# mLSTM values of two heads projected with tokens on partitions, the doubling operand of the delta-rule solve placed behind the low parts of the weights, longer pauses in the mixers

## Chip, cores and metric

One core of one Trainium2 chip runs the whole kernel. The metric is device time in microseconds (us) of one execution; the median of several runs is compared. TensorE (PE) does matmuls and transposes, VectorE (DVE), ScalarE (ACT) and GpSimd (POOL) do the element work, SyncE (SP) issues the DMAs.

## What is computed

One decoder layer on 1024 tokens of width 1024, all in float32: RMSNorm, one combined input projection, three causal token mixers in parallel (gated DeltaNet with 4 heads, mLSTM with 4 heads, native sparse attention with 8 heads), their output projections, merge gates, an output projection, a SwiGLU feed-forward part and a gated per-layer embedding. The part that the change touches most, the mLSTM of a head (cut):

```
qk = einsum('nbhid,nbhjd->nbhij', qc, kc)          # chunks of 64 tokens
Sm = exp(D_ - mt[..., None]) * qk_                 # decays and gates
num = si[..., None] * (q_ @ Cb) + Sm @ v_          # values v enter here
den = si * (q_ . nb) + sum(Sm, -1)
h  = num / max(|den|, exp(-mt))[..., None]
Cb = sc * Cb + wk^T @ v_                           # and here: state matrix
...
h = rms_f32(h, norm_w) * sigmoid(o_pre)
```

and of the gated DeltaNet the triangular solve `T = (I + X)^-1` with `u = T @ (v*beta)`, `w = T @ (k*beta*exp(g))`, the scan over chunks, and `rms_f32(o, norm_w) * silu(z)`.

## The kernel before

**Products.** A float32 product is made of three matmuls in a rounded float32 format: with each operand split into a high part and the rest (low part), high by high, high by low, low by high. The activations are split once per stage. The weights are streamed in blocks of four tiles of 128x512 (`run_blocks`, L404): SP fetches `wraw` two blocks ahead, ACT copies it to the high part `whi` (L434), POOL subtracts to get the low part `wlo` (L436), with five buffers for each. While block i is multiplied, the parts of block i+1 are made.

**Two forms of a block.** `chan_block` (L484) keeps a 128x128 piece of weights as the stationary operand and streams 512 tokens: the result has channels on partitions. A block is 2 column tiles x 2 halves of the tokens x 8 steps of the depth x 3 = 96 matmuls of 512 columns. `tok_block` keeps 128 tokens as the stationary operand and streams 256 columns of weights: the result has tokens on partitions, 8 token tiles x 8 x 3 = 192 matmuls of 256 columns. Both write to the two PSUM banks called `mm`, in turn, and an eviction empties a bank after each 24 matmuls.

**Mixers woven in.** Between two steps of a block (`advance`), generators of the mixers are moved on: `scans()` (`gdn_scan` of the four heads) and `side()` (the gates, `gdn_solve` of four heads, `mls_side` of four heads, with tables of the attention after the second). Each `yield` is such a place. `pause(us)` lets a generator sit out so much of woven time, in which the projections go on (a step counts 1.4 us). `behind()` ties a group of PE instructions behind the last matmul of the block so far. A scheduler then puts the instructions in order, so that the order on an engine is not simply that of the code.

**Stages of the profiled execution** (us): set-up to 60; DeltaNet heads' projections, with solves and scans beside them, to some 450; mLSTM heads to some 740; projections for the attention to 890; attention to 1290; branch and output projections to 1500; feed-forward and embedding to the end.

**What the change's steps touch.**
- `gates` side: `m_crow` (L749) is a running maximum on DVE; PE transposes it (`mtr2`; the trace writes `mtr`).
- `gdn_solve`: after the substitution on DVE, blocks of 16x16 go through DRAM (`xds`, L964, and back to `zd`, L967), and POOL spreads one of them into `gV` (L974), DVE the other into `gW`; then come the doubling steps on PE (`levq`, `levv`, `levw`).
- `gdn_scan`, its end: the sums of squares give `rsqrt` (a chain of tiny DVE operations on 128x8, L298 to L302), two DVE multiplications on `vtok` (L1078), a pause, two groups of four PE transposes (`gytr`), and DVE multiplies by the gate (L1085).
- `mls_blocks` (L1093): two channel blocks a head, (q, k) and (v, o), evicted by ACT (L1104, L1106).
- `mls_side` (L1113): row broadcasts `mrb` on PE from diagonals `mrb_d` that POOL makes (L813); `mE` is made by DVE (L1125), POOL (L1126) and ACT (exp, L1127), and multiplied on DVE (L1136) by `mqk` from PE; `mktr` are transposes of k, from which DVE makes `mwk` (L1141). The values come with channels on partitions, so PE transposes them in two groups of four (`mvtr`, L1147) and ACT copies the results to `mva` (L1149), which has a 129th column of ones. Then eight chunks of `mops` and `mups` (matmuls of 129 columns), the norm, a pause, and transposes `mytr`.

Of the kernel before, what the change touches and what calls it, by code (L numbers as in the profile page):

```python
# [11 lines left out]
F32 = mybir.dt.float32  # L12
F32R = mybir.dt.float32r
I32 = mybir.dt.int32
AF = mybir.ActivationFunctionType
# [121 lines left out]
def _blocks(w_in, w_branch, w_out, w_ffn_in, w_ffn_out, w_ple_gate, w_ple_proj):  # L137
    out = []

    def cols(w, *cs):  # L140
        out.append(np.concatenate([_rows(w[:, c:c + n]) for c, n in cs], 2).reshape(P, -1))
# [15 lines left out]
    for h in range(4):  # L157
        c = 2056 + 128 * h
        cols(w_in, (c, 128), (512 + c, 128))
        cols(w_in, (1024 + c, 128), (1536 + c, 128))  # L160
# [61 lines left out]
def bc(ap, shape):  # L222
    return ap.to_broadcast(list(shape))
# [8 lines left out]
class Trunk:  # L232
# [170 lines left out]
    def run_blocks(self, blocks, rate, both=0, first=None, fetch=None):  # L403
# [21 lines left out]
        def halve(i):  # L425
            if i < n:
                parts = self.raw.pop(i)
                if len(blocks[i]) > 2:
                    parts = blocks[i][2](parts)
                self.wsplit[i] = []  # L430
                for t in parts:
                    hi = self.wpool.tile([P, 512], F32R, tag="whi", name="whi", bufs=W_BUFS[1])
                    lo = self.wpool.tile([P, 512], F32R, tag="wlo", name="wlo", bufs=W_BUFS[1])
                    nc.scalar.activation(hi, t, AF.Copy)  # L434
                    eng = nc.vector if len(blocks[i]) == 2 and len(self.wsplit[i]) % 2 < both else nc.gpsimd
                    eng.tensor_tensor(lo, t, hi.bitcast(F32), OP.subtract)  # L436
                    self.wsplit[i].append((hi, lo))
# [235 lines left out]
    def gates_side(self):  # L673
# [76 lines left out]
        yield from self.pause(2.0)  # L750
# [113 lines left out]
    def gdn_solve(self, h):  # L864
# [107 lines left out]
        V, W = r3(self.b2("gV")), r3(self.b2("gW"))  # L972
        for eng, M, w in ((nc.gpsimd, V, 0), (nc.vector, W, 1)):
            eng.tensor_tensor(M.rearrange("p t (d i) -> p t d i", d=4), bc(d3(1 + w).unsqueeze(2), [P, NT, 4, 16]),  # L974
                              bc(self.blk4.unsqueeze(1).unsqueeze(3), [P, NT, 4, 16]), OP.mult)
        yield from self.pause(24.0)
# [50 lines left out]
    def gdn_scan(self, h):  # L1027
# [51 lines left out]
        yield from self.pause(8.0)  # L1079
# [13 lines left out]
    def mls_blocks(self, h):  # L1093
        nc = self.nc
        st = self.ml[h] = {}

        def evac(which):
            def f(ct, hf, ps):
                n = which[ct]
                sl = slice(hf * 512, hf * 512 + 512)  # L1100
                if hf == 0:
                    st[n] = self.a4("m" + n, tag="x")
                if n == "o":
                    nc.scalar.activation(st[n][:, sl], ps, AF.Tanh, scale=0.5)  # L1104
                else:
                    nc.scalar.activation(st[n][:, sl], ps, AF.Copy, scale=128 ** -0.5 if n == "k" else 1.0)  # L1106
                if hf == 1:
                    self.flags.add(("m", h, n))
            return f

        return [(self.chan_block(self.u, evac("qk")), None), (self.chan_block(self.u, evac("vo")), None)]

    def mls_side(self, h):  # L1113
        nc = self.nc
        st = self.ml[h]
# [13 lines left out]
        yield  # L1129
# [14 lines left out]
        va = self.a4("mva")[:, :].rearrange("p (t c) -> p t c", c=129)  # L1144
        nc.gpsimd.memset(va[:, :, 128:129], 1.0)
        for hf in H:
            with self.behind():  # L1147
                ps = self.four_tr(st["v"][:, hf * 512:hf * 512 + 512], "mvtr")
            nc.scalar.activation(va[:, 4 * hf:4 * hf + 4, 0:128], t4(ps[:, :]), AF.Copy)  # L1149
            yield  # L1150
# [38 lines left out]
        yield from self.pause(6.0)  # L1189
# [864 lines left out]
    def build(self, stages="ABCNRF"):  # L2054
# [23 lines left out]
        with tc.tile_pool(name="small", bufs=1) as self.spool, tc.tile_pool(name="mix", bufs=1) as self.apool, \  # L2078
                tc.tile_pool(name="halves", bufs=1) as self.bpool, tc.tile_pool(name="stage", bufs=2) as self.stage:
            self.setup()  # L2080
            with tc.tile_pool(name="ps1", bufs=1, space=MS) as self.psum:
# [5 lines left out]
                for h in range(4):  # L2087
                    blocks += self.mls_blocks(h)
# [52 lines left out]
```

## Time and profile before

| | |
|---|---|
| median of 3 runs | 2320.23 us (2319.97 to 2320.33) |
| the profiled execution, its own time | 2323.84 us |
| span of its trace | 2322.1 us |
| mean granted TensorE clock | 0.993 |
| PE busy | 2260.9 us, 97% of the span |
| DVE, ACT, POOL busy | 1325.0 (57%), 851.4 (37%), 732.2 (32%) |
| chain that ended last | PE 83%, DVE 11%, issue 3%, ACT 2%, others about 1% |

How to read it: the busy shares say which engine has the least room. The chain that ended last is followed back from the last instruction, at each step to what released it; its share of an engine is time that the end hangs on. The granted clock is the share of full speed that TensorE was given in a stretch; it has two levels, 1.2 and 2.4 GHz. A timeline row has the start, the length and the operation of a run of equal instructions; in brackets stands how long the engine sat idle before it and what released it. Starts of PE rows are exact to the hundredth shown; the ends are modelled and overlap the next row, so a rate on PE is read from start to start.

### The profile page before, as it was taken

What the parts mean: (1) busy time and instruction counts of PE and PEld (TensorE: products, weight loads), DVE (VectorE), ACT (ScalarE), POOL (GpSimd) and SP (SyncE); (2) the same over time, 40 slices, a digit from 0 to 9 for tenths busy, and PEclk for the clock granted to TensorE, in tenths of its full rate; (3) what the DMA queues carried; (4) which work ended last, traced back from release to release, by engine and by line L of the source; (5) the groups of instructions that cost most, each with busy time, mean ns of one, the idle gap of its engine ahead of it and who ended that gap; (6) DMA issues with size and microseconds to landing.
All of it is one profiled execution on the core that took longest, in us unless ns stands there. A gap on an engine that the chain in (4) does not pass through costs nothing.

```text
span 2322.1 us, 32707 instructions
## 1 busy us (share of the span) xinstructions
PE 2260.9 (97%) x12032; PEld 1796.5 (77%) x12032; DVE 1325.0 (57%) x3050; ACT 851.4 (37%) x1817; POOL 732.2 (32%) x616
## 2 busy tenths in 40 slices
PE   8999999999999999999999999999999999999999
PEld 6777778788778996667667777777888888888877
DVE  5445554644223446888883456587555555555584
ACT  6423232423322335555553323453222222222362
POOL 2343434332222123221222151214334444344412
PEclk9999999999999999999999999999999999999999
DMA  6130312121222132111103653311111111111134
GB/s 229 51 107 28 107 38 89 46 62 37 82 70 82 46 109 96 51 60 37 37 33 106 221 185 128 123 55 47 54 50 51 53 52 50 50 51 55 55 124 144
DMA packets 115111, 182.93 MB, mean 79 GB/s; under 512 B 24523, under 2 KB 34420, under 8 KB 114952
## 3 DMA queue, kind: packets, MB, share of 16 engines
q1 hardware_dynamic: 114664, 180.71, 22.9%
q8 instruction: 95, 1.56, 0.3%
q14 instruction: 64, 0.52, 0.1%
q10 hardware_dynamic: 288, 0.14, 0.0%
HBM read 149.04 MB, written 31.76 MB: 78 GB/s over the span
## 4 chain that ended last, share of the span: by engine, by line
PE 83%; DVE 11%; issue 3%; ACT 2%; DMA 1%; POOL 1%; SPq 0%; ACTq 0%; DVEq 0%; POOLq 0%
PE mm L247 67%; PE nso L247 3%; PE ptr L255 2%; PE S L247 2%; DVE P L1553 1%; PE mops L247 1%; PE gks L247 1%; PE gram L247 1%; PE gpu L247 1%; DVE P L1542 1%; POOL wlo L436 0%; DVE wlo L436 0%; DVE xn L1803 0%; DVE kT L852 0%; PE levv L247 0%
## 5 line engine op out<-in xcount | busy, mean ns | idle before, releaser
L436 POOL TENSOR_TENSOR wlo<-wraw,whi 128x512 fp32r<-128x512 f32 x334 | 446.8, 1344 | 1016.3 <-ACT whi L434 786.1
L247 PE MATMUL mm<-u,whi 128*128 128x512 f32 x1888 | 629.7, 408 | 3.9 <-ACT mg L1682 2.1
L434 ACT ACTIVATE whi<-wraw 128x512 fp32r<-128x512 f32 x408 | 255.9, 630 | 430.0 <-PE mm L247 339.5
L247 PEld LDWEIGHTS mm<-u,whi 128*128 128x128 f32 x1888 | 346.6, 191 | 77.4 <-issue 5.2
L247 PE MATMUL mm<-u,wlo 128*128 128x512 f32 x928 | 374.8, 404 | 3.6 <-POOL wlo L436 3.6
L247 PEld LDWEIGHTS mm<-u,wlo 128*128 128x128 f32 x928 | 176.0, 190 | 41.5 <-POOL wlo L436 4.1
L1921 DVE TENSOR_TENSOR fc<-fc,mm 128x512 f32<-128x512 f32 x140 | 95.2, 686 | 156.2 <-PE mm L247 156.2
L1962 DVE TENSOR_TENSOR xt<-xt,mm 128x512 f32<-128x512 f32 x176 | 118.2, 684 | 55.9 <-PE mm L247 54.6
L247 PE MATMUL mm<-whi,alo 128*128 128x512 f32 x352 | 140.7, 400 | 0.0
L247 PE MATMUL mm<-whi,ahi 128*128 128x512 f32 x352 | 139.8, 397 | 0.6 <-DVE xt L1962 0.5
L247 PE MATMUL mm<-wlo,ahi 128*128 128x512 f32 x352 | 139.5, 396 | 0.0
L436 POOL TENSOR_TENSOR wlo<-ws,whi 128x512 fp32r<-128x512 f32 x60 | 85.1, 1418 | 150.4 <-ACT whi L434 150.4
L247 PE MATMUL mm<-u2lo,whi 128*128 128x512 f32 x304 | 120.6, 397 | 0.0
L247 PE MATMUL mm<-u2hi,whi 128*128 128x512 f32 x304 | 120.3, 396 | 0.0
L247 PE MATMUL mm<-u2hi,wlo 128*128 128x512 f32 x304 | 119.7, 394 | 0.0
L436 DVE TENSOR_TENSOR wlo<-wraw,whi 128x512 fp32r<-128x512 f32 x74 | 68.7, 928 | 77.4 <-ACT whi L434 77.2
L1548 ACT ACTIVATE P<-P,n_ng 128x640 f32<-128x640 f32 (+7 forms) x128 | 92.8, 727 | 54.0 <-DVE n_ng L1546 53.5
L434 ACT ACTIVATE whi<-ws 128x512 fp32r<-128x512 f32 x60 | 37.8, 630 | 167.2 <-DVE xt L1962 114.7
L255 PE MATMUL ptr<-ident,P 128*128 128x128 f32 x528 | 88.2, 280 | 8.2 <-DVE P L1553 7.5
L247 PE MATMUL mm<-whi,u 128*128 128x256 f32 x512 | 94.3, 283 | 0.0
L255 PEld LDWEIGHTS ptr<-ident,P 128*128 128x128 f32 x528 | 60.6, 140 | 40.1 <-DVE P L1553 13.0
L247 PEld LDWEIGHTS mm<-whi,alo 128*128 128x128 f32 x352 | 66.3, 188 | 18.7 <-DVE alo L1878 3.1
(506 smaller groups left out, 4711.4 us busy)
## 6 DMA issues: line engine op xcount, KB each, us to landing
wraw<-in_w_dram SPq DMA_DIRECT2D x408, 256.0 KB, 2.5
mgs<-mg SPq DMA_DIRECT2D x48, 256.0 KB, 2.2
mgld<-mgs SPq DMA_DIRECT2D x48, 256.0 KB, 5.4
xt<-in_x_dram SPq DMA_DIRECT2D x8, 512.0 KB, 5.8
xt<-in_x_dram SPq DMA_DIRECT2D x16, 256.0 KB, 6.1
pg<-pps SPq DMA_DIRECT2D x16, 256.0 KB, 3.8
out_dram<-sg SPq DMA_DIRECT2D x15, 256.0 KB, 2.5
pps<-ppst SPq DMA_DIRECT2D x8, 256.0 KB, 2.0
```

The source lines that it names most:

```text
L247: return self.nc.tensor.matmul(out, lhsT, rhs, start=start, stop=stop).ins
L255: self.nc.tensor.transpose(out, in_, self.ident[:n, :n])
L434: nc.scalar.activation(hi, t, AF.Copy)
L436: eng.tensor_tensor(lo, t, hi.bitcast(F32), OP.subtract)
L1542: nc.vector.tensor_tensor_reduce(pt[:, farw:nk], sp2[:, farw - cut:nk - cut], near[g][:, n % 2], 1.0, -3e38, OP.add, OP.max, mx[:, n, 1:2])
L1548: nc.scalar.activation(pts[i][:, :nk], pts[i][:, :nk], AF.Exp, bias=ng[:, i:i + 1], accum_out=sm[:, g, i % 2:i % 2 + 1])
L1553: nc.vector.tensor_scalar(pts[i][:, :nk], pts[i][:, :nk], sm[:, g, i % 2:i % 2 + 1], gate[:, g, i % 2:i % 2 + 1], OP.mult, OP.mult)
L1921: nc.vector.tensor_tensor(t, x, ps, OP.add)
L1962: nc.vector.tensor_tensor(self.h[tt][s], self.h[tt][s], ps, OP.add)
```

## The change

- `mls_blocks` takes a pair of heads. Its blocks are (q, k of the first), (values of both), (o of both), (q, k of the second) in place of (q, k), (v, o), (q, k), (v, o). The values' block is a `tok_block`: tokens on partitions, 256 columns for two heads. Its results are copied by ACT straight into `mva` of either head, 128x128 each, two for a token tile. The transposes `mvtr` and the copies behind them are gone. The host's packing of the weights follows the same order.
- `run_blocks` remembers the last low part that POOL was given (`last_lo`), and `gdn_solve` issues `gV` behind it; its pause of 24 is split into 10 before `gV` and `gW`, and 14 after.
- Pauses: before the transposes of `m_crow` 2 to 5, before `gytr` 8 to 12, before `mqk` one step to 6, before `mytr` 6 to 11.

```diff
@@ -1,5 +1,5 @@
 import math
-from contextlib import ExitStack, contextmanager
+from contextlib import ExitStack, contextmanager, nullcontext
 
 import numpy as np
 
@@ -154,10 +154,12 @@
         cols(w_in, (1024 + c, 128), (1536 + c, 128))
         for b in _MG[h]:
             gates(b)
-    for h in range(4):
+    for h in (0, 2):
         c = 2056 + 128 * h
         cols(w_in, (c, 128), (512 + c, 128))
-        cols(w_in, (1024 + c, 128), (1536 + c, 128))
+        cols(w_in, (1024 + c, 256))
+        cols(w_in, (1536 + c, 256))
+        cols(w_in, (128 + c, 128), (640 + c, 128))
     for c in (4624, 4880, 5136, 4112, 4368):
         cols(w_in, (c, 256))
     for b in _MG[4]:
@@ -433,7 +435,9 @@
                     lo = self.wpool.tile([P, 512], F32R, tag="wlo", name="wlo", bufs=W_BUFS[1])
                     nc.scalar.activation(hi, t, AF.Copy)
                     eng = nc.vector if len(blocks[i]) == 2 and len(self.wsplit[i]) % 2 < both else nc.gpsimd
-                    eng.tensor_tensor(lo, t, hi.bitcast(F32), OP.subtract)
+                    low = eng.tensor_tensor(lo, t, hi.bitcast(F32), OP.subtract)
+                    if eng is nc.gpsimd:
+                        self.last_lo = low.ins
                     self.wsplit[i].append((hi, lo))
 
         self.raw, self.wsplit = {}, {}
@@ -747,7 +751,7 @@
         nc.vector.tensor_copy(srow, ps[:32, :P])
         crow = self.b2("m_crow")[:32, :P]
         nc.vector.tensor_tensor_scan(crow, srow, srow, -3e38, OP.max, OP.max)
-        yield from self.pause(2.0)
+        yield from self.pause(5.0)
         ps = self.ps("mtr2")
         with self.behind():
             self.tr(ps[:, :32], crow)
@@ -970,10 +974,14 @@
         ch = lambda m, c: m[64 * (c % 2):64 * (c % 2) + 64, c // 2]
         r3 = lambda t: t[:, :].rearrange("p (t c) -> p t c", c=64)
         V, W = r3(self.b2("gV")), r3(self.b2("gW"))
+        yield from self.pause(10.0)
         for eng, M, w in ((nc.gpsimd, V, 0), (nc.vector, W, 1)):
-            eng.tensor_tensor(M.rearrange("p t (d i) -> p t d i", d=4), bc(d3(1 + w).unsqueeze(2), [P, NT, 4, 16]),
-                              bc(self.blk4.unsqueeze(1).unsqueeze(3), [P, NT, 4, 16]), OP.mult)
-        yield from self.pause(24.0)
+
+            with self.tc.issue_after(self.last_lo) if w == 0 else nullcontext():
+                eng.tensor_tensor(M.rearrange("p t (d i) -> p t d i", d=4),
+                                  bc(d3(1 + w).unsqueeze(2), [P, NT, 4, 16]),
+                                  bc(self.blk4.unsqueeze(1).unsqueeze(3), [P, NT, 4, 16]), OP.mult)
+        yield from self.pause(14.0)
 
         VV = t4(self.a4("gVV")[:, :S])
         nc.gpsimd.memset(VV[64:128, :, 0:64], 0.0)
@@ -1076,7 +1084,7 @@
         for hf in H:
             sl = slice(hf * 512, hf * 512 + 512)
             nc.vector.tensor_tensor(t4(o[:, sl]), t4(o[:, sl]), hd(f, hf), OP.mult)
-        yield from self.pause(8.0)
+        yield from self.pause(12.0)
         yT = self.a4("gyT")
         for hf in H:
             sl = slice(hf * 512, hf * 512 + 512)
@@ -1091,28 +1099,41 @@
 
 
     def mls_blocks(self, h):
-        nc = self.nc
-        st = self.ml[h] = {}
-
-        def evac(which):
+
+
+        nc = self.nc
+        st = [self.ml.setdefault(h + i, {}) for i in range(2)]
+
+        def evac(names):
             def f(ct, hf, ps):
-                n = which[ct]
+                n, i = names[ct]
                 sl = slice(hf * 512, hf * 512 + 512)
                 if hf == 0:
-                    st[n] = self.a4("m" + n, tag="x")
+                    st[i][n] = self.a4("m" + n, tag="x")
                 if n == "o":
-                    nc.scalar.activation(st[n][:, sl], ps, AF.Tanh, scale=0.5)
+                    nc.scalar.activation(st[i][n][:, sl], ps, AF.Tanh, scale=0.5)
                 else:
-                    nc.scalar.activation(st[n][:, sl], ps, AF.Copy, scale=128 ** -0.5 if n == "k" else 1.0)
+                    nc.scalar.activation(st[i][n][:, sl], ps, AF.Copy, scale=128 ** -0.5 if n == "k" else 1.0)
                 if hf == 1:
-                    self.flags.add(("m", h, n))
+                    self.flags.add(("m", h + i, n))
             return f
 
-        return [(self.chan_block(self.u, evac("qk")), None), (self.chan_block(self.u, evac("vo")), None)]
+        def values(tt, _, ps):
+            for i in range(2):
+                if tt == 0:
+                    va = st[i]["v"] = self.a4("mva")[:, :].rearrange("p (t c) -> p t c", c=129)
+                    nc.gpsimd.memset(va[:, :, 128:129], 1.0)
+                nc.scalar.activation(st[i]["v"][:, tt, 0:128], ps[:, i * P:i * P + P], AF.Copy)
+                if tt == NT - 1:
+                    self.flags.add(("m", h + i, "v"))
+
+        chan = lambda *names: (self.chan_block(self.u, evac(names)), None)
+        return [chan(("q", 0), ("k", 0)), (self.tok_block(self.utok, values), None), chan(("o", 0), ("o", 1)),
+                chan(("q", 1), ("k", 1))]
 
     def mls_side(self, h):
         nc = self.nc
-        st = self.ml[h]
+        st = self.ml.setdefault(h, {})
         H = range(2)
         t4 = lambda ap: ap.rearrange("p (t c) -> p t c", c=P)
         hd = lambda ap, hf: bc(ap[:, 4 * hf:4 * hf + 4].unsqueeze(2), [P, 4, P])
@@ -1126,7 +1147,7 @@
             nc.gpsimd.tensor_tensor(t4(E), t4(E), bc(self.cmask.unsqueeze(1), [P, 4, P]), OP.add)
             nc.scalar.activation(E, E, AF.Exp)
             sms.append(E)
-        yield
+        yield from self.pause(6.0)
         for hf in H:
             ps = self.ps("mqk")
             with self.behind():
@@ -1141,13 +1162,7 @@
             nc.vector.tensor_tensor(t4(wk[:, hf * 512:hf * 512 + 512]), t4(ps[:, :]), hd(self.mwks[:, :, h], hf), OP.mult)
             yield
         yield from self.need(("m", h, "v"))
-        va = self.a4("mva")[:, :].rearrange("p (t c) -> p t c", c=129)
-        nc.gpsimd.memset(va[:, :, 128:129], 1.0)
-        for hf in H:
-            with self.behind():
-                ps = self.four_tr(st["v"][:, hf * 512:hf * 512 + 512], "mvtr")
-            nc.scalar.activation(va[:, 4 * hf:4 * hf + 4, 0:128], t4(ps[:, :]), AF.Copy)
-            yield
+        va = st["v"]
         C = self.small("mC", [P, 129], bufs=2)
         nc.gpsimd.memset(C, 0.0)
         num = self.a4("mnum")[:, :].rearrange("p (t c) -> p t c", c=129)
@@ -1186,7 +1201,7 @@
         for hf in H:
             sl = slice(hf * 512, hf * 512 + 512)
             nc.vector.tensor_tensor(t4(y[:, sl]), num[:, 4 * hf:4 * hf + 4, 0:128], hd(f, hf), OP.mult)
-        yield from self.pause(6.0)
+        yield from self.pause(11.0)
         yT = self.a4("myT")
         for hf in H:
             sl = slice(hf * 512, hf * 512 + 512)
@@ -2084,7 +2099,7 @@
                 for h in range(4):
                     blocks += self.gdn_blocks(h)
                     blocks += [self.mg_block(b, 0) for b in _MG[h]]
-                for h in range(4):
+                for h in (0, 2):
                     blocks += self.mls_blocks(h)
                 blocks += self.nsa_blocks()
                 blocks += [self.mg_block(b, 0) for b in _MG[4]]
```

In the changed file the same lines stand 2 to 15 lines lower. How it moves instructions is shown at three places.

POOL, at the first solve's `gV`, before. The four tiles `wlo_1444` to `wlo_1456` are the low parts of one block of weights, `wlo_1524` the first of the next:

```order
L436 TENSOR_TENSOR wlo_1444<-wraw_1316,whi_1443 128x512 [waits DMAHW0_49,PE_49,Activation_49]
L436 TENSOR_TENSOR wlo_1448<-wraw_1318,whi_1447 128x512 [waits DMAHW4_49,PE_49,Activation_49]
L436 TENSOR_TENSOR wlo_1452<-wraw_1320,whi_1451 128x512 [waits DMAHW5_49,PE_49,Activation_49]
L974 TENSOR_TENSOR gV_1424<-zd_1366,c128_135 128x512 [waits DMAHW3_49]
L436 TENSOR_TENSOR wlo_1456<-wraw_1322,whi_1455 128x512 [waits DMAHW6_49,PE_49,Activation_49]
L436 TENSOR_TENSOR wlo_1524<-wraw_1459,whi_1523 128x512 [waits DMAHW0_49,PE_49,Activation_49]
L813 TENSOR_TENSOR gcb_d_1780<-ident_87,cumhi_785 128x512 [waits DVE_49,PE_49]
```

and with the change (there the four are `wlo_1442` to `wlo_1454`):

```order
L438 TENSOR_TENSOR wlo_1442<-wraw_1316,whi_1441 128x512 [waits DMAHW0_49,PE_49,Activation_49]
L438 TENSOR_TENSOR wlo_1446<-wraw_1318,whi_1445 128x512 [waits DMAHW4_49,PE_49,Activation_49]
L438 TENSOR_TENSOR wlo_1450<-wraw_1320,whi_1449 128x512 [waits DMAHW5_49,PE_49,Activation_49]
L438 TENSOR_TENSOR wlo_1454<-wraw_1322,whi_1453 128x512 [waits DMAHW6_49,PE_49,Activation_49]
L981 TENSOR_TENSOR gV_1424<-zd_1366,c128_135 128x512 [waits DMAHW3_49]
L438 TENSOR_TENSOR wlo_1524<-wraw_1457,whi_1523 128x512 [waits DMAHW0_49,PE_49,Activation_49]
L817 TENSOR_TENSOR gcb_d_1780<-ident_87,cumhi_785 128x512 [waits DVE_49,PE_49]
```

The fourth low part now goes ahead of `gV`, which waits for a DMA in both orders.

PE, at the end of the first head's scan, before. `mm_2157` and `mm_2234` are projection banks, `ktr` transposes of the next head:

```order
L247 MATMUL mm_2157<-u_600,whi_1535 128x512 x2
L247 MATMUL mm_2157<-u_600,wlo_1536 128x512
L247 MATMUL mm_2157<-u_618,whi_1535 128x512 x2
L247 MATMUL mm_2157<-u_618,wlo_1536 128x512
L255 MATMUL gytr_2198<-ident_87,vtok_1757 128x128 [waits DVE_49,Activation_49]
L255 MATMUL gytr_2198<-ident_87,vtok_1757 128x128 x3
L255 MATMUL gytr_2204<-ident_87,vtok_1757 128x128 [waits DVE_49]
L255 MATMUL gytr_2204<-ident_87,vtok_1757 128x128 x3
L247 MATMUL mm_2234<-u_301,whi_1874 128x512 x2
```

with the change (the end of what now goes ahead of `gytr`; `mm_2221` is the bank after `mm_2157`, and three of its triples of matmuls and the first matmul of a fourth stand before this piece):

```order
L257 MATMUL ktr_2176<-ident_87,gq_1912 128x128 [waits Activation_49]
L257 MATMUL ktr_2176<-ident_87,gq_1912 128x128 x3
L249 MATMUL mm_2221<-u_334,whi_1878 128x512
L249 MATMUL mm_2221<-u_334,wlo_1879 128x512
L249 MATMUL mm_2221<-u_382,whi_1882 128x512 x2
L249 MATMUL mm_2221<-u_382,wlo_1883 128x512 [waits Pool_49]
L249 MATMUL mm_2221<-u_390,whi_1882 128x512 x2
L249 MATMUL mm_2221<-u_390,wlo_1883 128x512
L257 MATMUL gytr_2262<-ident_87,vtok_1757 128x128 [waits DVE_49]
L257 MATMUL gytr_2262<-ident_87,vtok_1757 128x128 x3
L257 MATMUL gytr_2268<-ident_87,vtok_1757 128x128 [waits DVE_49]
L257 MATMUL gytr_2268<-ident_87,vtok_1757 128x128 x3
```

Between the last matmul of `mm_2157` and the first `gytr` there was nothing, and now there are 18 matmuls of the next bank and the four `ktr` transposes. At the second head 21 matmuls and four transposes are moved ahead in the same way.

PE, at the running maximum in the gates' side, before:

```order
L255 MATMUL mtr_804<-ident_87,m_s_802 32x128 [waits DVE_49,Activation_49]
L247 MATMUL mm_848<-u_468,wlo_639 128x512
L247 MATMUL mm_848<-u_486,whi_638 128x512 x2
L247 MATMUL mm_848<-u_486,wlo_639 128x512
L255 MATMUL mtr2_825<-ident_87,m_crow_808 128x32 [waits DVE_49,PE_49]
L247 MATMUL mm_848<-u_504,whi_642 128x512 x2
L247 MATMUL msel_829<-m_cmx_827,cset_140 128x32 [waits DVE_49,Activation_49]
```

and with the change:

```order
L257 MATMUL mtr_804<-ident_87,m_s_802 32x128 [waits DVE_49,Activation_49]
L249 MATMUL mm_825<-u_468,wlo_639 128x512
L249 MATMUL mm_825<-u_486,whi_638 128x512 x2
L249 MATMUL mm_825<-u_486,wlo_639 128x512
L249 MATMUL mm_825<-u_504,whi_642 128x512 x2
L249 MATMUL mm_825<-u_504,wlo_643 128x512
L249 MATMUL mm_825<-u_522,whi_642 128x512 x2
L249 MATMUL mm_825<-u_522,wlo_643 128x512
L257 MATMUL mtr2_838<-ident_87,m_crow_808 128x32 [waits DVE_49,PE_49]
L249 MATMUL mm_825<-u_540,whi_646 128x512 x2
L249 MATMUL msel_842<-m_cmx_840,cset_140 128x32 [waits DVE_49,Activation_49]
```

Six more matmuls of 512 columns stand ahead of the transpose of `m_crow`.

## Rows read from the trace of the kernel before

**Rows 1.** The page's busy line of PE, and its chain that ended last by engine.

```profile
PE 2260.9 (97%) x12032; PEld 1796.5 (77%) x12032; DVE 1325.0 (57%) x3050; ACT 851.4 (37%) x1817; POOL 732.2 (32%) x616
PE 83%; DVE 11%; issue 3%; ACT 2%; DMA 1%; POOL 1%; SPq 0%; ACTq 0%; DVEq 0%; POOLq 0%
```

**Rows 2.** Waits of PE from 60 to 740 us, by the waiting operation and what released it. Columns: total us, times, longest us.

```profile
PE gytr L255 <- DVE vtok L1078: 5.4, 2, 3.1
PE mm L247 <- POOL wlo L436: 3.6, 1, 3.6
PE mtr L255 <- DVE m_tmp L765: 2.9, 1, 2.9
PE mvtr L255 <- DVE mE L1136: 2.1, 1, 2.1
PE gpu L247 <- DVE gvn L1053: 1.9, 3, 0.9
```

**Rows 3.** Windows of the span: length, then busy us of PE, PEld, DVE, ACT, POOL with the number of instructions, the granted clock (PEclk), DMA share, GB/s. The first five hold one long idle of PE each; the last two are the mLSTM stage and a stretch of token blocks in the attention's projections.

```profile
70.00:90.00 20.00, 17.13 (x66) 13.53 (x66) 10.92 (x36) 4.73 (x13) 8.71 (x8) 0.83 0.00 1
160.00:180.00 20.00, 16.38 (x157) 12.59 (x157) 2.67 (x4) 1.19 (x2) 4.01 (x4) 0.91 0.30 87
230.00:250.00 20.00, 16.92 (x77) 13.54 (x77) 10.20 (x26) 8.98 (x32) 9.61 (x10) 0.91 0.32 116
340.00:360.00 20.00, 17.66 (x78) 14.40 (x77) 12.89 (x35) 9.04 (x35) 10.04 (x10) 0.91 0.27 100
660.00:680.00 20.00, 17.86 (x102) 14.66 (x101) 6.82 (x17) 7.87 (x17) 7.88 (x8) 0.91 0.26 91
450.00:740.00 290.00, 286.71 (x1619) 230.91 (x1618) 112.74 (x307) 89.13 (x192) 85.66 (x81) 0.99 0.20 65
759.00:850.00 91.00, 87.94 (x834) 85.90 (x833) 42.29 (x112) 32.41 (x81) 17.72 (x16) 1.00 0.23 75
```

**Rows 4.** Timeline of PE in a channel block (512 columns) and in a token block (256 columns): start, length, operation, count.

```profile
466.62 0.63 PE L247 MATMUL mm<-u,whi 128*128 128x512 f32 x2
...
468.72 0.62 PE L247 MATMUL mm<-u,whi 128*128 128x512 f32 x2
...
771.09 0.40 PE L247 MATMUL mm<-whi,u 128*128 128x256 f32 x2
...
773.22 0.40 PE L247 MATMUL mm<-whi,u 128*128 128x256 f32 x2
```

**Rows 5.** Timeline of PE at one group of `mvtr` and the two projection rows behind it.

```profile
546.34 0.60 PE L255 MATMUL mvtr<-ident,mv 128*128 128x128 f32 x4
546.70 0.72 PE L247 MATMUL mm<-u,whi 128*128 128x512 f32 x2
547.25 0.39 PE L247 MATMUL mm<-u,wlo 128*128 128x512 f32 x1
```

**Rows 6.** Groups of ACT instructions by tile: count, ns least/median/most, first and last start. The copies that the change drops, and 128x128 copies from a bank of a token block in the attention's projections.

```profile
L1149 ACT ACTIVATE mva<-mvtr x8: 590/598/601, 544.7 to 715.2; 128x512 f32<-128x512 f32 x8
L1228 ACT ACTIVATE nvs<-mm x8: 260/278/278, 765.1 to 788.6; 128x128 f32<-128x128 f32 x8
```

**Rows 7.** Timelines at the first `gV`: ACT, POOL, PE.

```profile
157.53 0.63 ACT L434 ACTIVATE whi<-wraw 128x512 fp32r<-128x512 f32 x1 [0.76 <-PE mm L247]
163.14 1.04 POOL L974 TENSOR_TENSOR gV<-zd,c 128x512 f32<-128x512 f32 x1 [6.34 <-DMA zd<-xds]
164.14 3.00 POOL L436 TENSOR_TENSOR wlo<-wraw,whi 128x512 fp32r<-128x512 f32 x2
165.95 0.50 PE L247 MATMUL mm<-u,wlo 128*128 128x512 f32 x1 [3.62 <-POOL wlo L436]
```

**Rows 8.** Timelines at the end of the first scan: four rows of DVE, then one of POOL.

```profile
230.59 0.17 DVE L300 TENSOR_TENSOR rsq_tgo<-rsq_ygo 128x8 f32<-128x8 f32 x1
230.79 1.13 DVE L301 SCALAR_TENSOR_TENSOR rsq_tgo<-rsq_tgo,g_s 128x8 f32<-128x8 f32 x1
...
231.96 1.19 DVE L302 SCALAR_TENSOR_TENSOR rsq_ygo<-rsq_tgo,rsq_ygo 128x8 f32<-128x8 f32 x1
...
233.38 1.29 DVE L1078 TENSOR_TENSOR vtok<-vtok,rsq_ygo 128x512 f32<-128x512 f32 x2
...
230.62 2.51 POOL L436 TENSOR_TENSOR wlo<-wraw,whi 128x512 fp32r<-128x512 f32 x2 [0.28 <-ACT whi L434]
```

**Rows 9.** Timelines at the running maximum (DVE), and of PE after another idle time, in the set-up.

```profile
74.44 1.26 DVE L749 TENSOR_TENSOR_SCAN m_crow<-m_srow 32x128 f32<-32x128 f32 x1
34.23 0.65 PE L255 MATMUL trx<-ident,xt 128*128 128x128 f32 x4 [1.70 <-DVE u L325]
...
34.95 0.40 PE L247 MATMUL mm<-wlo,pThi 128*128 128x512 f32 x1
35.19 0.39 PE L247 MATMUL mm<-whi,pTlo 128*128 128x512 f32 x1
```

**Rows 10.** Timelines at the third mLSTM head: POOL, ACT, DVE.

```profile
666.30 1.26 POOL L1126 TENSOR_TENSOR mE<-mE,c 128x512 f32<-128x512 f32 x1
...
667.60 0.63 ACT L1127 ACTIVATE mE<-mE 128x512 f32<-128x512 f32 x1 [2.15 <-POOL mE L1126]
668.26 0.69 DVE L1136 TENSOR_TENSOR mE<-mqk,mE 128x512 f32<-128x512 f32 x1 [2.36 <-ACT mE L1127]
```

**Rows 11.** Timeline of PE at the change from one token block to the next in the attention's projections.

```profile
790.49 0.39 PE L247 MATMUL mm<-wlo,u 128*128 128x256 f32 x1 [0.25 <-POOL wlo L436]
```

## The prediction

> **What bounds the kernel now.** First the page: PE is busy for 97% of the span, and 83% of the chain that ended last is PE [rows 1]. So the time goes down only where PE has less to do, where it stops waiting, or where it runs at a higher clock. Second, the waits of PE in the part of the program that the change touches, 60 to 740 us [rows 2]: four kinds carry most of it, `gytr` 5.4 us in two waits (3.1 the longer one, so 2.3 the other), a projection matmul that waits 3.6 us for a low part from POOL, the transpose of `m_crow` 2.9 us, the first `mvtr` of the third mLSTM head 2.1 us. Third, the granted clock around these waits [rows 3]. The first five windows of 20 us each hold one of them, and in all five the mean clock is below full: 0.83 around the `m_crow` wait, 0.91 around the others. A clock of 0.83 over 20 us is 0.17 x 20 = 3.4 us of PE work not done; 0.91 is 0.09 x 20 = 1.8 us. Since TensorE has two levels, this is a stretch at 1.2 GHz behind each wait. The reader should see that such a wait costs its own length and then 1.8 to 3.4 us more. An idle time of 1.70 us in the set-up was not followed by this: from 34.95 to 35.19 a 512-column matmul takes 0.24 us [rows 9], the full rate of rows 4.
>
> **The change, part by part.** Each term stands against the profiled execution of 2323.84 us, which is 3.6 us above the median of the runs; I take the sum off the median.
>
> *Transposes of the values.* Eight groups of `mvtr` go (two a head). From start to start a group takes 546.70 - 546.34 = 0.36 us [rows 5]; the next pair of matmuls starts its successor 0.55 us later, where two matmuls at the rate of rows 4 take 0.47, so a group costs 0.36 to 0.445. Eight are 2.9 to 3.6; I take **-3.2**. The ACT copies are off the path: 8 copies to `mva` of 598 ns and as many evictions to `mv` give way to 32 of 278 ns [rows 6], 9.6 against 8.9 us, with ACT busy for 89 of 290 us in that stage [rows 3].
>
> *Token blocks in place of channel blocks.* Nine 512-column matmuls take 468.72 - 466.62 = 2.10 us, eighteen of 256 columns 773.22 - 771.09 = 2.13 us [rows 4]. A channel block is 96 x 0.2333 = 22.40 us, a token block 192 x 0.1183 = 22.72: +0.32 for each of the two. At its start a token block takes up the four weight tiles twice as fast; where one token block follows another PE waited 0.25 us for the low part [rows 11]. I add that at both: **+1.1** (0.6 to 2.1).
>
> *`gV` behind the low parts.* POOL stood idle 6.34 us for `zd` until 163.14, then made `gV` until 164.18, and the fourth low part of the running block only after it; PE waited for it until 165.95, 3.62 us [rows 7]. The high part it needs was there at 157.53 + 0.63 = 158.16. In the new order the low part goes first, so it is there about 1.4 us after that, near 159.6 (two take 3.00 us [rows 7]), before PE asks at 165.95 - 3.62 = 162.33. The wait goes, and with it the low clock of that window: -3.6 - 1.8 = **-5.4**. Behind `gV` on POOL stands the next block's first low part, which PE asks for only after a quarter of the running block more; the doubling steps that read `gV` and `gW` are paced by 24 us of woven projections in all, before and after. So I cost the later `gV` at nothing; without that cover it would be its own 1.04 us.
>
> *`gytr`.* The DVE chain of the norm ends with two multiplications started at 233.38, and PE waits for the first until 234.22. With the change 18 matmuls (4.2 us) and four transposes (about 0.45, as a little more than a group of rows 5) stand ahead: 4.65 us against a wait of 3.1, a margin of 1.6. At the second head it is 21 matmuls and four transposes, 5.3 us against 2.3. Both waits go, and both low clocks: -3.1 - 2.3 - 1.8 - 1.8 = **-9.0**. The parts of the next bank that are now asked for earlier are made in time: the third and fourth low part run from 230.62 to 233.13 [rows 8], and PE, which stands free from 231.1, would come to them at about 234 and 237. The DVE steps behind (the multiplication by the gate) move behind the next head's key norm; nobody waits soon.
> Here the trace shows a cause that the change leaves in place. A DVE operation on 128x8 takes 0.17 us, but 1.13 and 1.19 where POOL makes a low part at the same time [rows 8]. The Trainium skill, "SBUF — State Buffer", section "SBUF: two separate sides", says that the port pair of VectorE and GpSimd is an exclusive lock, held for a whole instruction, against VectorE operations with two SBUF inputs. The trace agrees: the slow operation from 231.96 ends at 233.15, the low part beside it at 233.13. By that rule the chain can still grow where two more of its operations meet POOL, by some 2.0 us: 0.4 us of waiting would come back at the first head and the sum would be -19.4 in place of -19.8.
>
> *`m_crow`.* The scan on DVE ends at 74.44 + 1.26 = 75.70 [rows 9], and nothing of the change makes it earlier. Six more matmuls, 1.4 us, go ahead of the transpose: the wait shrinks from 2.87 to about 1.5 us. Unless the clock falls behind it, another 3.4 go [rows 3]. The nearest rows are 1.70 us without a fall [rows 9] and 2.1 with one [rows 2, 3], and 1.5 lies below both: -1.4 - 3.4 = **-4.8**; if it falls, -1.4.
>
> *Third mLSTM head.* Here `mvtr` waited, but not for values: its bank is that of `mqk`, which the second DVE multiplication (668.26) frees [rows 10]. That one waits for the exp (2.36 us), this for POOL's second `mE` (2.15 us), which stands behind other POOL work. With `mvtr` gone the first `mops` takes that bank and waits for the same multiplication. The order gives two more projection matmuls ahead of it (0.5 us), but takes away nothing of the chain, and puts a low part (1.5 us [rows 7]) where one of two diagonals stood between the two `mE` on POOL. The new pause of 6 lies elsewhere here. I take the wait as staying, with its low clock: **+0.5** (-3.9 if all goes, +1.1 at worst).
>
> *The other pauses* (`mqk`, `mytr`) remove next to nothing that the waits show. New small waits: the relaxed order makes other neighbours, the scans' steps in a token block above all. The nearest row is `gpu`, 1.9 us in three waits [rows 2]; I take **+1.0** (0 to 4).
>
> Sum: -3.2 + 1.1 - 5.4 - 9.0 - 4.8 + 0.5 + 1.0 = -19.8; 2320.23 - 19.8 = **2300.4 us**.
>
> **Rivals.**
> *The waits shrink but the low clock stays.* If the 1.5 us at `m_crow` is still followed by a fall (+3.4), the norm's chain keeps a remnant of 0.4 us at the first head, and the clock still falls at both heads (+0.4 + 3.6), the third mLSTM head is at its worst (+0.6) and the small waits are at 4 (+3.0), the sum is -8.8: 2311.4. For it: all five long waits had a fall. Against: 1.70 us had none, and four of the five should be gone or under that. Chance 0.18.
> *The fourth low part is late anyway.* `gV` moves, but the low part waits for something else (its buffer, the copy). Then 5.4 come back: 2305.8. Against: the high part was ready 4 us before PE asked. Chance 0.05.
> *Slower: evictions of the values' block.* In a token block a bank must be emptied within 24 x 0.1183 = 2.84 us, and ACT takes its work in order. An exp that ACT waits for holds the copies: it stood 2.15 us before one [rows 10]. If the copies of all 16 token tiles came late enough for PE to wait 1.5 us each, that is +24, and two low clocks in each of the two blocks add 7.2: 2300.4 + 31 = 2331. It decides where ACT's delay behind a finished tile, its own two copies (0.56) included, passes 2.84 us regularly. Against: the attention's token blocks, with the same turnover, had PE busy for 87.94 of 91.00 us at clock 1.00 [rows 3]. Chance 0.04.
>
> **How the numbers follow.** The forecast has a chance of 0.73; its own range is 2294 to 2306: down to it if the third head's wait goes after all (-4.4 against +0.5), the groups cost 3.6 and no small wait comes, up to it with the fall at `m_crow` and a little more. To take in the first rival I go to 2313. What measures as different from no change is 0.2%, 4.6 us: faster means under 2315.6. All of the forecast and of the second rival lies there, and most of the first; I leave 0.07 for outcomes near no change, and 0.05 for slower, the third rival and what like it I did not see. Faster 0.88.
>
> **What would show it.** In the profile after: no `mvtr`; 192 matmuls of 256 columns in each values' block in some 22.7 us; the fourth low part ahead of `gV` and no PE wait of 3.6 us near 162; `gytr` without a wait at the first two heads; a wait of 1.5 at the `m_crow` transpose at most; the granted clock of the first four windows near 1.00; a wait of about 2 to 3 us at the first `mops` of the third head, with 0.9 behind it. The prediction is wrong if waits of over 2 us stand at new places in the mixers, or if PE waits for banks in the values' blocks.

## The result, and the profile after

The changed kernel takes 2305.45 us (median of 4 runs, 2303.08 to 2309.02), the kernel before 2320.28 (2319.97 to 2320.38): ratio 0.9932, interval [0.992, 0.9944], 14.8 us less. 2300.4 was forecast, with 2294 to 2313 as the range. The profiled execution took 2305.59 us, its span is 2303.9, the mean granted clock 0.998; PE is busy for 2249.7 us (98%).

The waits of PE from 60 to 740 us, the view of [rows 2], after:

```profile
PE mops L249 <- DVE mE L1157: 1.9, 1, 1.9
PE mops L249 <- DVE mC L1178: 1.5, 1, 1.5
PE gks L249 <- DVE gS L1068: 1.5, 2, 1.0
PE mtr L257 <- DVE m_tmp L769: 1.5, 1, 1.5
PE mm L249 <- ACT nksq L1245: 1.0, 1, 1.0
PE gpu L249 <- DVE gvn L1061: 0.9, 2, 0.7
...
PE mops L249 <- DVE rsq_tgo L302: 0.4, 1, 0.4
```

The waits at `gytr` and for the low part are gone, the transpose of `m_crow` waits 1.5 us for 2.9, and the third mLSTM head still waits 1.9 us, at `mops` now. New are two waits of `mops` (1.5 and 0.4) and the one behind `nksq`, an eviction in the attention's first token block. The clock around the same places, the columns of [rows 3]:

```profile
70.00:90.00 20.00, 18.51 (x82) 14.57 (x82) 10.82 (x32) 7.22 (x16) 11.82 (x11) 1.00 0.04 14
155.00:175.00 20.00, 20.00 (x236) 15.88 (x235) 6.29 (x8) 1.19 (x2) 5.04 (x5) 1.00 0.34 93
225.00:245.00 20.00, 20.00 (x113) 17.08 (x112) 13.14 (x27) 5.89 (x12) 10.18 (x10) 1.00 0.32 110
335.00:355.00 20.00, 20.00 (x113) 17.10 (x112) 12.78 (x21) 6.78 (x12) 11.79 (x11) 1.00 0.38 122
665.00:685.00 20.00, 18.11 (x106) 15.15 (x105) 7.94 (x23) 7.53 (x16) 7.54 (x8) 0.91 0.17 57
```

Full clock where the first four waits stood in [rows 3], and 0.91 behind the one that stayed. How far the work has come shows where the time went. Groups of PE by tile, first and last start, before (first two rows) and after: `khtr` ends the DeltaNet heads' solves, `S` begins the attention.

```profile
L255 PE MATMUL khtr<-ident,khat x32: 270/272/273, 129.3 to 470.2; 128*128 128x128 f32 x32
L247 PE MATMUL S<-khh,qT x192: 222/364/527, 891.9 to 1226.3; 128*128 128x256 f32 x64, 128*128 128x384 f32 x64, 128*128 128x512 f32 x48, 128*128 128x128 f32 x16
```

```profile
L257 PE MATMUL khtr<-ident,khat x32: 270/272/273, 124.1 to 450.4; 128*128 128x128 f32 x32
L249 PE MATMUL S<-khh,qT x192: 220/363/505, 872.6 to 1207.2; 128*128 128x256 f32 x64, 128*128 128x384 f32 x64, 128*128 128x512 f32 x48, 128*128 128x128 f32 x16
```

At the end of the solves the changed kernel is 19.8 us ahead, at the start of the attention 19.3, at the end of the span 18.2. Of this, 1.0 was there before the first edit, at the gates' first transposes (71.8 us before, 70.7 after). The windows from there to the end of the solves, and on to the start of the attention, before and after:

```profile
71.77:470.18 398.41, 383.50 (x2347) 310.47 (x2346) 220.20 (x442) 136.21 (x366) 156.42 (x142) 0.98 0.20 66
470.18:891.85 421.67, 414.29 (x2789) 351.58 (x2787) 157.65 (x414) 127.44 (x271) 110.00 (x101) 1.00 0.22 72
```

```profile
70.74:450.41 379.67, 375.07 (x2346) 304.60 (x2345) 221.32 (x442) 136.06 (x366) 155.85 (x142) 1.00 0.22 68
450.41:872.58 422.17, 412.63 (x2949) 358.64 (x2948) 159.74 (x414) 125.20 (x287) 109.89 (x102) 1.00 0.23 73
```

The length less the busy time of PE (the first two numbers) is its idle time. In the DeltaNet part the stretch is 18.7 us shorter, with 4.6 us idle for 14.9; in the mLSTM stage and the projections behind it, it is 0.5 longer, with 9.5 us idle for 7.4. So all of the gain behind the set-up lies in the DeltaNet part; the mLSTM stage gives nothing. And the profiled executions differ by 18.2 us where the medians differ by 14.8. Both points are what the runs below are about.

### The profile page after: what moved, and what is told of

It reads as the page before. It is cut to its first block, busy times and chain, and to the rows that moved or that the text cites. A ratio compares the mean times of both kernels' runs of the same rounds, so it can differ in the third digit from the quotient of the medians.

```text
span 2303.9 us, 33036 instructions
## 1 busy us (share of the span) xinstructions
PE 2249.7 (98%) x12192; PEld 1795.9 (78%) x12192; DVE 1327.5 (58%) x3050; ACT 848.7 (37%) x1833; POOL 730.3 (32%) x616
## 4 chain that ended last, share of the span: by engine, by line
PE 83%; DVE 9%; issue 4%; ACT 2%; DMA 1%; POOL 1%; SPq 0%; DVEq 0%; ACTq 0%; POOLq 0%
PE mm L249 67%; PE nso L249 3%; PE ptr L257 2%; PE S L249 2%; DVE P L1568 1%; PE mops L249 1%; PE gks L249 1%; PE gram L249 1%; PE gpu L249 1%; POOL wlo L438 1%; DVE P L1557 1%; DVE xn L1818 0%; DVE kT L856 0%; PE levv L249 0%; PE levq L249 0%
## 5 line engine op out<-in xcount | busy, mean ns | idle before, releaser
L249 PE MATMUL mm<-u,whi 128*128 128x512 f32 x1760 | 586.6, 407 | 3.5 <-ACT mg L1697 2.0
L249 PEld LDWEIGHTS mm<-u,whi 128*128 128x128 f32 x1760 | 320.6, 189 | 68.5 <-issue 3.5
L249 PE MATMUL mm<-u,wlo 128*128 128x512 f32 x864 | 346.9, 401 | 0.0
L249 PEld LDWEIGHTS mm<-u,wlo 128*128 128x128 f32 x864 | 162.9, 189 | 34.2 <-issue 1.0
L249 PE MATMUL mm<-whi,u 128*128 128x256 f32 x768 | 144.3, 285 | 2.8 <-ACT nksq L1245 2.7
L249 PEld LDWEIGHTS mm<-whi,u 128*128 128x128 f32 x768 | 119.7, 188 | 7.3 <-ACT nksq L1245 3.5
L249 PE MATMUL mm<-wlo,u 128*128 128x256 f32 x384 | 108.4, 282 | 0.8 <-POOL wlo L438 0.8
```

The lines of the kernel that those rows point to most:

```text
L249: return self.nc.tensor.matmul(out, lhsT, rhs, start=start, stop=stop).ins
```

## Experiments

Each run is compared with the kernel before on its own chip (medians 2320.49 to 2320.64 us); e1 to e4 ran on one chip, e5 to e8 on a second, e9, i3 and i4 on a third.

**One part at a time, on the kernel before.** e1: only the values' projection (block order, `tok_block`, no `mvtr`).

```diff
-                for h in range(4):
+                for h in (0, 2):
                     blocks += self.mls_blocks(h)
...
-            with self.behind():
-                ps = self.four_tr(st["v"][:, hf * 512:hf * 512 + 512], "mvtr")
+        va = st["v"]
```

> Only the values' projection of the change: token blocks for two heads, no transposes of the values, the new order of blocks; POOL's order around the operand of the solve and all pauses as before. Theory (every part is worth what its rows say): 8 groups of transposes go (-3.2), token blocks cost 1.1, the third mLSTM head's wait stays (+0.5), so -1.6 +- 1.5, about 2318.7. Rival (the new order of the mLSTM stage makes new waits: in the changed kernel a chunk of the first mLSTM head waits 1.5 us for VectorE, and the attention's token blocks wait 2.7 us for ScalarE where it was 0.8): 0 to +3, 2320 to 2323.

2326.51 us, ratio 1.0029 [1.0018, 1.0039]: **slower by 6.0**, more than the rival said. Waits of PE from 60 to 880 us, two rows:

```profile
PE mytr L257 <- DVE my L1197: 7.2, 5, 2.8
...
PE gks L249 <- DVE m_oss L1189: 1.4, 1, 1.4
```

With the o blocks of a pair moved and the values made elsewhere, the last transposes of a head come right behind its norm on DVE: 7.2 us of waits where before there were 0.2. Alone, this part loses.

e2: only the operand of the solve.

```diff
+        yield from self.pause(10.0)
...
+            with self.tc.issue_after(self.last_lo) if w == 0 else nullcontext():
...
-        yield from self.pause(24.0)
+        yield from self.pause(14.0)
```

> Only the operand of the solve behind the low parts, with its pause split in 10 and 14. Theory: the wait of 3.6 us near 162 us goes, with 1.8 us of low clock behind it: -5.4, about 2314.9, and the profile has full clock from 160 to 180 us. Rival (the low clock behind a wait is not there in every execution, so that the profile shows more than the median gains): -3.6, 2316.7.

2318.51 us, ratio 0.9985 [0.9977, 0.9994]: 2.0 us less, a smaller gain than either reading. The wait near 162 us and its low clock are gone (second of the windows below), but the attention's tables now wait 2.8 us for a DMA. One row of its waits, and four windows:

```profile
PE nearps L247 <- DMA relflip<-relscr: 2.8, 1, 2.8
```

```profile
70.00:90.00 20.00, 17.11 (x67) 13.50 (x67) 10.91 (x36) 4.72 (x12) 8.69 (x8) 0.83 0.00 1
155.00:175.00 20.00, 20.00 (x182) 15.93 (x182) 7.08 (x12) 3.58 (x6) 6.20 (x6) 1.00 0.33 93
335.00:355.00 20.00, 17.66 (x88) 14.37 (x87) 12.78 (x35) 10.06 (x37) 11.53 (x12) 1.00 0.33 115
660.00:680.00 20.00, 17.84 (x114) 14.57 (x113) 7.89 (x21) 6.46 (x14) 6.79 (x8) 1.00 0.12 42
```

e3: only the pause ahead of `gytr`, and e4: only that ahead of the transpose of `m_crow`.

```diff
-        yield from self.pause(8.0)
+        yield from self.pause(12.0)
```

```diff
-        yield from self.pause(2.0)
+        yield from self.pause(5.0)
```

> Only the pause ahead of the scans' transposes, 8 to 12. Theory: two waits go, 3.1 and 2.3 us, and two falls of the clock of 1.8 us each: -9.0, about 2311.3. Rival (the low clock is not there in every execution): -5.4 to -7, 2313.3 to 2314.9.

> Only the pause ahead of the transpose of the running maximum, 2 to 5. Theory: the wait goes from 2.9 to 1.5 us and the clock no longer falls behind it (3.4 us): -4.8, about 2315.5. Rival 1 (the clock still falls in a part of the executions, or falls for only 1.8 us in most executions of the kernel before): -1.4 to -3.2, 2317.1 to 2318.9, with executions that differ by 1.8 or 3.4 us among themselves.

e3: 2314.19 us, ratio 0.9972 [0.996, 0.9983], 6.4 less, where the theory said 9.0 and the rival 5.4 to 7. e4: 2317.66, ratio 0.9989 [0.998, 0.9998], 2.9 less, between 1.4 and 4.8; its runs lie from 2315.68 to 2322.26. In both the rival's range holds, and the profiles fit its reason; in e3 the wait of `mvtr` at the third mLSTM head grew as well, from 2.1 to 2.9 us, which takes 0.8 off its gain. A window of e4 and the row of the wait in it, then one of e3 with the untouched `m_crow` wait of 2.88 us:

```profile
335.00:355.00 20.00, 17.64 (x87) 14.31 (x86) 12.24 (x33) 10.86 (x38) 11.53 (x12) 1.00 0.34 121
```

```profile
341.98 0.63 PE L255 MATMUL gytr<-ident,vtok 128*128 128x128 f32 x4 [2.36 <-DVE vtok L1078]
```

```profile
70.00:90.00 20.00, 17.12 (x71) 13.59 (x71) 10.92 (x36) 5.33 (x13) 8.73 (x8) 0.91 0.00 1
```

The second head's wait of 2.36 us stands in e4 as before, at full clock; so it does in e2, above. In the profile before it had 0.91 [rows 3]. The `m_crow` wait has 0.83 before and in e2 (3.4 us), 0.91 in e3 (1.8). The third mLSTM head's `mvtr` waits 2.14 us before and in e2, with 0.91 before [rows 3] and 1.00 in e2 (the last of its windows). **The same wait, to 0.1 us, is followed by a low clock in one execution, by a shorter one or by none in another.** The wait of 3.1 at the first head and that of 3.6 to 3.8 for the low part had theirs in every profile that I have with them.

**Undo one part of the changed kernel.** e5: the pause ahead of `mytr` back to 6. e6: one step ahead of `mqk`. e7: the values as before, all else changed. e8: the changed kernel again.

```diff
-        yield from self.pause(11.0)
+        yield from self.pause(6.00)
```

```diff
             sms.append(E)
-        yield from self.pause(6.0)
+        yield
```

> The changed kernel with the pause ahead of `mytr` back at 6. Theory (with the values' projection moved, the last transposes of a head come close behind the norm on VectorE, and this pause covers it; without it they waited 7.2 us in five waits in the run of the values' projection alone): +5 to +8 against the changed kernel, 2310 to 2313, with waits at `mytr` at two heads at least. Rival (those waits came from the order of that run alone): +0 to +1, about 2306.

> The changed kernel with one step ahead of `mqk` in place of the pause of 6. Theory (this pause covers nothing that the waits of the kernel before show): within 1.5 us of the changed kernel, 2304 to 2307. Rival (it spreads the mLSTM head's start, and without it `mqk` and `mops` wait for VectorE at more heads than the third): +3 to +5, 2308 to 2310.

> All of the change but the values' projection: operand of the solve behind the low parts, all four pauses; values with channels on partitions and their transposes as before. Theory of the prediction (the values' projection is worth 1.6 us where the pauses cover it): 2307. Rival 1 (it is worth nothing or costs, since the mLSTM stage of the changed kernel has new waits of 1.5 and 2.7 us): 2302 to 2305. Rival 2 (the pauses bring their gain only with it): 2310 or more.

> The changed kernel again, unchanged. Theory (the low clock behind a wait is there in one execution and not in another): its executions differ by steps of about 1.7 us, between 2303 and 2309, and a second profile shows the low clock at other places than the first (670 and 938 us), with the same waits to 0.1 us. Rival (executions differ in their waits): waits of other lengths or at other places.

e8 took 2303.88 us, ratio 0.9929 [0.9917, 0.9942]: 16.6 less than the kernel before on that chip, where the first runs gave 14.8. e5: 2303.92, 0.9932 [0.992, 0.9945], no difference, as its rival said: `mytr` waits 2.3 us in three waits there, but the 2.7 us of waits behind `nksq` are gone. e7: 2308.09, 0.9953 [0.9941, 0.9966]: beside the pauses the values' projection is worth 4.2 us, more than forecast. From the end of the solves to the start of the attention e7 takes 426.1 us and e8 422.3, with PE idle for 10.3 and 9.5. So the waits, `mvtr` at the third head with 3.4 us among them, make 0.8 of it, and PE's busy time about 3.0, where the sum had 2.1 for the transposes less the token blocks. e6: **2300.31, 0.9913 [0.99, 0.9927]**, 3.6 us faster than e8, with all five executions below those of e8: the pause ahead of `mqk` costs. Both readings expected no gain; none foresaw this sign. Waits of PE from 60 to 880 us, e8 and then e6:

```profile
PE mm L249 <- ACT nksq L1245: 2.7, 3, 1.2
PE mops L249 <- DVE mE L1157: 1.9, 1, 1.9
PE mops L249 <- DVE mC L1178: 1.5, 1, 1.5
```

```profile
PE mops L249 <- DVE mE L1157: 2.1, 1, 2.1
...
PE gks L249 <- DVE m_oss L1195: 1.4, 1, 1.4
```

The same stretch, from the end of the solves to the start of the attention, in e8 and then in e6:

```profile
450.19:872.44 422.25, 412.73 (x2949) 358.82 (x2947) 160.08 (x414) 125.28 (x287) 109.99 (x102) 1.00 0.22 73
450.05:868.81 418.76, 410.81 (x2949) 359.37 (x2948) 161.42 (x414) 125.30 (x287) 111.26 (x102) 1.00 0.22 74
```

It is 3.5 us shorter in e6, with 8.0 us idle for 9.5. The pause pushes the mLSTM heads later: the last `mytr` starts at 743.0 us in e8 and at 734.6 in e6. In e8 an eviction in the attention's token blocks stands on DVE behind the multiplications of the last head's norm, and a projection matmul waits 1.0 us for it; two rows of DVE, one of PE:

```profile
737.19 1.29 DVE L1203 TENSOR_TENSOR my<-mnum,rsq_ymo 128x512 f32<-128x512 f32 x2
738.40 0.28 DVE L1242 COPY nks<-mm 128x128 f32<-128x128 f32 x1
```

```profile
739.27 0.39 PE L249 MATMUL mm<-whi,u 128*128 128x256 f32 x1 [1.01 <-ACT nksq L1245]
```

The other two waits behind `nksq` (at 770.79 and 778.21 us) stand behind steps of the attention's own keys on DVE, which come later too (the last `ncmp` starts at 762.9 us in e8 and at 755.6 in e6). The first head's chunks come behind the last scan's norm: in the changed kernel the chunk's DVE step stands behind two multiplications of that norm:

```profile
549.05 1.29 DVE L1086 TENSOR_TENSOR vtok<-vtok,rsq_ygo 128x512 f32<-128x512 f32 x2
550.26 0.34 DVE L1178 SCALAR_TENSOR_TENSOR mC<-mC,m_sc,mups 128x129 f32<-128x129 f32 x1
```

The idle time makes some 1.5 of the 3.5 us. The other 2 are in PE's busy time, for the same number of matmuls; which of them take longer, no run isolates.

e8 also gives the repeat: the waits agree with the first profile to 0.1 us, but that one had a low clock at 935 us, and this one none. A low clock that comes and goes was expected; but the one at the third head stayed, and the five executions lie within 2.1 us, without clear steps. From 930 to 945 us, the changed kernel's first profile and e8:

```profile
930.00:945.00 15.00, 12.90 (x71) 8.79 (x69) 12.89 (x49) 7.16 (x20) 4.50 (x5) 0.89 0.23 72
```

```profile
930.00:945.00 15.00, 12.89 (x77) 8.83 (x76) 13.58 (x54) 7.75 (x21) 4.50 (x5) 1.00 0.21 72
```

**The tie within the whole, and two repairs.** e9: the changed kernel with `gV` as before. i3: e6 with a pause of 26 ahead of `mqk` at the third head. i4: i3 with 8 for 5 at `m_crow`.

```diff
             sms.append(E)
-        yield from self.pause(6.0)
+        if h == 2:
+            yield from self.pause(26.0)
+        else:
+            yield
```

> The changed kernel with the operand of the solve as it was: not tied behind the low parts, its pause of 24 in one piece. Theory of the prediction (the tie is worth the wait of 3.6 us and 1.8 us of low clock): 2309 to 2310. Rival (as in the run of the tie alone, which gained 2.0 us, the wait comes back in part at another place): 2305 to 2306.

> The changed kernel with one step ahead of `mqk` at three heads and a pause of 26 at the third. Theory (at the third head the order of PE runs some 20 us of woven time behind the code, since the attention's tables in front wait for a DMA, so that a pause of 6 there does nothing, and one of 26 puts projection matmuls between `mqk`, `mktr` and `mops`): against the kernel with one step everywhere (2300.3) the wait of 2.1 us at the first `mops` of the third head goes, with the low clock behind it: -2 to -4, 2296 to 2298. Rival (the wait only moves to the end of that head, whose last transposes come 7 us later, or into the next head): 2300 +- 1.

> The same with the pause ahead of the transpose of the running maximum at 8 in place of 5. Theory (12 more matmuls of 512 columns, 2.8 us, stand ahead of it, and the wait of 1.5 us that was left goes): -1.5 against the run beside it, 2294.5 to 2296.5. Rival (the next steps of the gates come later and the first solve or scan waits for them): 0.

e9: 2306.57 us, 0.9939 [0.9925, 0.9952]: 2.7 above e8, in between theory and rival; a wait of 3.09 us is back at 161.72 with its low clock. All five executions of e9 lie above those of e8, so the tie gains, but their ranges on two chips (2305.39 to 2307.94 and 2302.60 to 2304.69) leave its size open by some 2 us either way. i3: 2297.39, 0.99 [0.9886, 0.9913], 2.9 less than e6 as the theory said; no wait of `mops` is left. i4: **2295.35 us, 0.9891 [0.9877, 0.9904]**, another 2.0 less: the best version, 8.5 us under e8. Its longest lines of waits from 60 to 880 us:

```profile
PE gks L249 <- DVE gS L1068: 1.5, 2, 1.0
PE khtr L255 <- ACT khht L1345: 1.4, 2, 0.8
PE gks L249 <- DVE m_oss L1198: 1.4, 1, 1.4
```

## Why the prediction was right, and by how much it was off

*The DeltaNet part* was forecast at -5.4 - 9.0 - 4.8 = -19.2, of which 10.4 were waits and 8.8 low clock. In the profile it is -18.7: 10.3 of idle time, and nearly all of the rest low clock that is gone. Waits and clock went as each step said, the 1.5 us left at `m_crow` too, and that without a low clock.

*The mLSTM stage*, with the projections behind it, was forecast at -3.2 + 1.1 + 0.5 + 1.0 = -0.6 and gave +0.5. PE is busy for 1.7 us less there, where 2.1 was forecast. The third head's wait stayed, as said (1.9 for 2.1, with 0.91). Mis-sized was the term of the new small waits: taken as 1.0, it is 2.3. New are 1.5 + 0.4 at `mops` and 2.7 at the evictions; gone are 0.9 at `gpu`, 0.8 at `ncmp` and 0.6 at `khtr`. And the step "the other pauses remove next to nothing" is true and not enough: the pause ahead of `mqk` costs 3.6 us (e6). With one step there the changed kernel takes 2300.31.

*Profile and median.* The step that was off by the most is taking a sum made on one profiled execution, clock and all, off the median of other executions. The execution before that was profiled stood 3.6 us above its median, at a mean clock of 0.993. Of 25 other executions of the kernel before, on the chip of e1 to e4, the four at 0.993 or less took 2321.84 to 2325.36 us, and the fifteen at 0.995 or more 2317.81 to 2322.14. So executions differ by their low clock, and part of what the sum counted as gain was low clock that the median execution does not have. The set-up, which no edit touches and no term counts, differs in this way too: before, and after,

```profile
10.00:60.00 50.00, 41.97 (x218) 33.66 (x217) 32.79 (x70) 30.86 (x56) 11.37 (x12) 0.93 0.63 221
```

```profile
10.00:60.00 50.00, 41.97 (x220) 33.46 (x219) 33.12 (x71) 31.15 (x57) 11.45 (x12) 0.97 0.65 225
```

0.07 x 50 = 3.5 us of low clock against 1.5, a part of it in idle time: the lead of 1.0 us at the gates, which is in the 18.2, comes from there. In the other runs this window has 0.90 to 0.97, whatever the edit. Of the two waits of the DeltaNet part whose low clock varies, `m_crow` had 3.4, 3.4, 1.8 and 1.8 in the four profiles with it untouched (before, e2, e1, e3), a mean of 2.6; the second head's `gytr` 1.8, 0, 0, 0 (before, e1, e2, e4), a mean of 0.45. With these the sum is -19.8 + 0.8 + 1.35 = -17.6, and with +0.5 for -0.6 in the mLSTM stage about -16.5. The first runs gave -14.8, with an interval from -18.6 to -13.0, and e8 -16.6. So the two corrections make 3.3 of the 5.0 us that the forecast was off, and what is left is within the spread. They were made after the fact, from few profiles, and no run tests their sizes.

*The rivals.* "The waits shrink but the low clock stays" did not come: four of five windows are at 1.00. What came is its mirror: the low clock had not always been there. The evictions of the values' blocks, the rival on the slower side, made no wait; the late evictions are those of the attention's blocks. The rule that the port pair of VectorE and GpSimd is locked for a whole instruction (the Trainium skill, "SBUF — State Buffer", "SBUF: two separate sides") allowed a longer DVE chain. The trace agrees that the slow operations are still there (1.22 us for the last of them, at 221.33), but the chain has not grown: from its first slow operation to the first multiplication of `vtok` it takes 5.97 us (from 216.82), where it took 5.90 (from 227.48), and `gytr` does not wait.

*Interaction.* e1 to e4 add to +6.0 - 2.0 - 6.4 - 2.9 = -5.3, the whole is -14.8. The values' projection is +6.0 on the old pauses and -4.2 beside the new ones, and e5 shows that the pause of 11 isn't needed where that of 6 ahead of `mqk` stands. Either longer pause seems to cover most of the waits at `mytr` (7.2 us in e1, 2.3 in e5, 0.2 in e6), and I had costed both at nothing because the kernel before had no such wait. The values' projection with one longer pause and nothing else was not run.

## What to carry to other kernels

Here a wait of TensorE of 2 to 4 us cost its length and, in some executions, 1.8 to 3.4 us of low clock; before that is counted as a gain, look at the same wait in several profiles, and at how the profiled execution stands to the median. A part that removes work can lose alone, as here, most likely because what it shortens was the cover of a wait: price it with the pacing that goes with it. And a pause in the code need not move the engine: at the third head a wait of 1.9 us stood with a pause of 6 and one of 2.1 without it, and 26 removed it. That the scheduler's order runs some 20 us behind the code there is the reason that I expected; no view here shows it.

## What the runs showed of the hardware

The granted clock behind a wait differs between executions of one kernel with the same waits: 1.00 or 0.89 from 930 to 945 us in two profiles of the changed kernel, where PE waits 0.9 to 1.1 us at a time. A wait of 2.8 us at `nearps` (e2) had no low clock. One of 1.9 us at the third head had 0.91 in both profiles of the changed kernel, and one of 2.1 us there had 0.91 in the kernel before and 1.00 in e2.
